# Working the borders between stages in two halves of 128 tokens

## The chip, the cores and the metric

The kernel runs on one core of one Trainium2 chip. The metric is the device time of one execution in microseconds (us); the lower, the better. TensorE multiplies matrices, VectorE (DVE), ScalarE (ACT) and GpSimd (POOL) work elementwise, SyncE (SP) issues the transfers.

## What is computed

The reference is a chain of transformer blocks in float32 on 256 tokens of 1024 channels, with 256 context tokens beside them in the first layer and a half. Cut to what matters here:

```python
def mod_norm(x, m, i, g):
    return rms_norm(x, g) * (1 + m[:, 3 * i + 1, None]) + m[:, 3 * i, None]
def swiglu(h, w1, w2):
    a, b = jnp.split(h @ w1, 2, axis=-1)
    return (jax.nn.silu(a) * b) @ w2
def ffn_sublayer(x, m, i, g, w1, w2):
    return x + HALF_STEP * m[:, 3 * i + 2, None] * swiglu(mod_norm(x, m, i, g), w1, w2)
...
        x = x + m[:, 5, None] * y
        x = ffn_sublayer(x, m, 2, norm_g[l, 2], ffn_w_in[l, 1], ffn_w_out[l, 1])
    return rms_norm(x, final_g)
```

So every stage ends with an output map that adds to the residual x, and the next one begins with a norm of x over its channels and a map of the normed values. After the second layer's last feed-forward part x is normed by `final_g` and normed again by the second block, whose residual is the normed x: this is the doubled norm below. A second block (retention and sparse attention) and a product-key expert layer follow.

## The kernel before

Tokens are the columns of a tile and channels its partitions: x is `X`, eight tiles of 128 channels by T tokens, where T is 512 (256 tokens and 256 of the context) up to the second layer's mixer, and 256 from there on. A linear map goes by output tiles of 128 channels. For each, the 128x1024 weights (a unit) come through the class `Stream`: `load` (L234) issues the transfer on SP, `split` (L240) makes two float32r parts of it, a copy on ScalarE (L252) and a subtraction on VectorE or POOL (L256, L254), and `take` and `next` hand it out. `take` also sets the mark (`busy`) behind which split buffers are free again. `mm3` (L296) issues three matmuls for each 128x128 block of weights: high part by high part of the input (L298), high by low (L299), low by high (L300). So an output tile is 24 matmuls with 8 blocks of weights, and each matmul loads its 128x128 weights anew. Engines work off their instructions in the order in which the program issues them; no scheduler reorders them.

Between two stages stands what is called a border here. `tail` (L716) works the eight output tiles of a stage and evacuates each into x (`evac`, L727: x plus gate times PSUM). Where the tail is the last of its stage, `sq` (L601) squares each x tile on ScalarE (L613) and POOL adds the squares up (L615), `stats` (L617) sums them over the channels by float32 matmuls with one moving column (L623, L624), `rpow` (L645) takes the power -1/2 on VectorE and POOL, `bcast` (L638) spreads the result over the partitions by a 128x128 matmul (L643), and `chunks` (L668) makes the normed input of the next map for each channel tile: `ht` (L659, VectorE), `Hh` (L661, ScalarE), `Hl` (L664, VectorE). Then `group` (L676) starts the next map's first three or four output tiles together, channel tile by channel tile, so that TensorE can begin as soon as the first chunk is there.

With T = 512, `tail` runs the tiles 5 to 7 in two halves of 256 tokens and puts the first half's statistics, broadcast and chunks beside the matmuls of the second; `group` does the same with the second half's. With T = 256 there are no halves: after the eighth tile the branch at L760 splits the units ahead, squares tile 7, and issues statistics, broadcast and all eight chunks one after another; `group` runs one pass of 256 columns.

Three borders have T = 256. The first goes from the second layer's mixer output map (eight blocks of input) to its feed-forward part (three tiles in the group; two more split buffers, m0 and m1, are there). The second goes from the last output map of that feed-forward part (seven blocks) to the second block's mixer (three tiles), with the doubled norm: `sq` squares each tile twice, `stats` takes two powers one after the other, and each chunk also rescales x (L663). The third goes from the second block's output map (eight blocks) to the expert layer's queries (four tiles). In the second and third there are five split buffers.

The branch for T = 256 at the end of `tail`, and the loop of `group`:

```python
        if T == 256:
            W.busy = W.pos
            W.split(W.pos + 4)
            W.load(W.pos + 6)
            self.sq(7)
            self.stats(0)
            self.bcast(0)
            self.chunks(0, 0, KD)
            return
...
        for half in range(T // S):
            if half == T // S - 1:
                W.split(W.pos + W.split_ahead)
```

Of the kernel before, what the change touches and what calls it, by code (L numbers as in the profile page):

```python
# [16 lines left out]
P = 128  # L17
# [269 lines left out]
class Build:  # L287
# [13 lines left out]

    def x_(self, T, d, half=None):
        return self.X[:, :, d, :] if T == 512 and half is None else self.X[:, half or 0, d, :]

    def h_(self, T, k, half=None):
        return [H[:, :, k, :] if T == 512 and half is None else H[:, half or 0, k, :] for H in (self.Hh, self.Hl)]

    def g_(self, T, k, half=None):
        c = slice(0, T) if half is None else slice(half * S, half * S + S)
        return [G[:, k, c] for G in (self.Gh, self.Gl)]  # L310

    def bank_(self, b, T, half=None):
        if isinstance(b, tuple):
            b, half = b
        return self.bank[b][:, :T] if half is None else self.bank[b][:, half * S:half * S + S]
# [285 lines left out]
    def sq(self, d, half=None):  # L601
        nc, T = self.nc, self.nT
        x = self.x_(T, d, half)
        sl = slice(0, T) if half is None else slice(half * S, half * S + S)
        jobs = [(sl, 1.0)]
        if self.ndouble:
            jobs.append((slice(S, 2 * S), self.gn[:, 48 + d:49 + d]))
# [9 lines left out]
    def stats(self, half):  # L617
        nc = self.nc
        st = self.bank[6][:, half * 8:half * 8 + 4]
        nset = 4 if self.ndouble else 2  # L620
        for j in range(nset):
            c0 = half * S + j * P
            nc.tensor.matmul(st[:, j:j + 1], self.nacc[:, c0:c0 + P], self.C["ones"][:, 0:1], start=True, stop=False)  # L623
            nc.tensor.matmul(st[:, j:j + 1], self.nlast[:, c0:c0 + P], self.C["ones"][:, 0:1], start=False, stop=True)  # L624
        ms = self.sm.tile([P, 8], F32, name="ms", tag="ms")
        r = self.sm.tile([P, 8], F32, name="rstd", tag="rstd")
        self.rpow(r[:, 0:2], ms[:, 0:2], st[:, 0:2], 1.0 / D)
        order = [0, 1]
        if self.ndouble:
            nc.vector.tensor_tensor(ms[:, 2:4], r[:, 0:2], r[:, 0:2], OP.mult)  # L630
            nc.vector.tensor_tensor(ms[:, 4:6], ms[:, 2:4], st[:, 2:4], OP.mult)
            self.rpow(r[:, 2:4], ms[:, 6:8], ms[:, 4:6], 1.0 / D)
            nc.vector.tensor_tensor(r[:, 2:4], r[:, 2:4], r[:, 0:2], OP.mult)
            order = [2, 3, 0, 1]
        R = self.bank[7]
        self.nrow[half] = R[:, half * S:half * S + S], [r[:, o:o + 1] for o in order]

    def bcast(self, half):  # L638

        R, cols = self.nrow[half]  # L640
        rows = [R[:, :P], R[:, P:]] + ([self.bank[7][:, S + j * P:S + (j + 1) * P] for j in range(2)] if self.ndouble else [])
# [9 lines left out]
    def chunk(self, half, k):  # L651
# [5 lines left out]
        t = self.np.tile([P, S], F32, name="ht", tag="ht", bufs=3)  # L657
# [4 lines left out]
        if self.ndouble:  # L662
            nc.vector.scalar_tensor_tensor(x, x, self.gn[:, 48 + k:49 + k], self.bank[7][:, S:], op0=OP.mult, op1=OP.mult)  # L663
# [10 lines left out]


    def group(self, labels, T, early=False):  # L676
# [7 lines left out]
        for half in range(T // S):  # L684
            if half == T // S - 1:
                W.split(W.pos + W.split_ahead)
            for k in range(KD):
# [4 lines left out]
                if T == 512 and half == 0:  # L692
# [3 lines left out]
                    if k == 5:  # L696
                        if not early:
                            self.bcast(1)
                        self.chunks(1, 0, KD)
        return bs  # L700
# [15 lines left out]
    def tail(self, label, nk, T, gate, last=True, order=None, rest=None):  # L716
# [3 lines left out]
        def evac(b, d, half):  # L720
# [5 lines left out]
            g = gate(half or 0)  # L726
# [15 lines left out]
        nfull = 5 if last and T == 512 else 8  # L742
# [1150 lines left out]
```

## Time and profile before

| what | value |
|---|---|
| median of 3 runs | 2723.25 us (2722.06 to 2727.45) |
| the profiled execution: its time | 2724.21 us |
| the profiled execution: span of its instructions | 2722.3 us |
| TensorE busy | 97% of the span |
| weight loads busy | 85% |
| VectorE, ScalarE, POOL busy | 65%, 40%, 19% |
| mean granted TensorE clock | 0.991 |

The span is read in the trace from the first instruction to the last; the 1.9 us between it and the time of the same execution lie around it. Matmuls are pipelined and their ends are modelled, so what a matmul costs is read from the distance between the starts of two of them. In a timeline row the numbers are start and length in us, then engine, line, operation, output and input, weights (rows*columns), moving operand (partitions x columns), and in brackets the idle time of the engine before it and what ended it.

### The profile page before, as it was taken

How to read it: one execution, taken by the hardware profiler on the slowest of the kernel's cores; microseconds unless marked ns; L12 is line 12 of the kernel's file. 1: busy time of each engine (PE TensorE's matmuls, PEld its weight loads, DVE VectorE, ACT ScalarE, POOL GpSimd, SP SyncE). 2: the span in 40 equal slices, each digit the busy share in tenths (PEclk: the TensorE clock that was granted, in tenths of full speed). 3: DMA queues.
4: the chain of work that ended last, by engine and by line, in shares of the span. 5: the costliest groups of instructions: out<-in, count | busy, mean ns of one | idle time of the engine just before them, and what ended most of it. 6: DMA issues, size and time to landing. Idle time of an engine off the chain costs nothing. (4 is left out here: it accounts for less than half of the span.)

```text
span 2722.3 us, 40945 instructions
## 1 busy us (share of the span) xinstructions
PE 2639.4 (97%) x15899; PEld 2312.6 (85%) x15899; DVE 1759.6 (65%) x3389; ACT 1102.2 (40%) x1867; POOL 507.7 (19%) x284
## 2 busy tenths in 40 slices
PE   6999999999999999999998999989999999999998
PEld 4888888688888898888978999778999999988887
DVE  6877865557777565555546656775795566655555
ACT  5322234534222242222354445553444545454554
POOL 1000011120000010000122001332697666300000
PEclk9999999999999999999999999999999999999999
DMA  6655643234566535655344655524555444566664
GB/s 246 200 188 182 205 151 111 67 101 140 193 189 194 182 124 186 203 190 194 108 149 130 191 188 172 174 75 160 171 165 169 151 151 148 157 196 204 193 193 140
DMA packets 129476, 451.40 MB, mean 166 GB/s; under 512 B 16000, under 2 KB 21120, under 8 KB 127744
## 3 DMA queue, kind: packets, MB, share of 16 engines
q1 hardware_dynamic: 129280, 448.77, 51.4%
q8 instruction: 125, 2.05, 0.3%
q14 instruction: 71, 0.58, 0.1%
HBM read 446.35 MB, written 2.10 MB: 165 GB/s over the span
## 5 line engine op out<-in xcount | busy, mean ns | idle before, releaser
L298 PE MATMUL bank<-Hh,hl 128*128 128x256 f32 (+1 forms) x1968 | 661.4, 336 | 9.4 <-ACT Hh L661 5.1
L300 PE MATMUL bank<-Hh,hl 128*128 128x256 f32 (+1 forms) x1968 | 639.9, 325 | 4.1 <-POOL hl L254 4.1
L299 PE MATMUL bank<-Hl,hl 128*128 128x256 f32 (+1 forms) x1968 | 640.4, 325 | 0.8 <-DVE Hl L664 0.7
L252 ACT ACTIVATE hl<-raw 128x1024 fp32r<-128x1024 f32 (+1 forms) x401 | 410.9, 1041 | 276.4 <-DMA raw<-in_w_dram 84.1
L256 DVE TENSOR_TENSOR hl<-raw,hl 128x1024 fp32r<-128x1024 f32 (+1 forms) x316 | 383.1, 1222 | 180.2 <-ACT hl L252 177.2
L298 PEld LDWEIGHTS bank<-Hh,hl 128*128 128x128 f32 x1968 | 375.8, 191 | 48.5 <-issue 7.7
L300 PEld LDWEIGHTS bank<-Hh,hl 128*128 128x128 f32 x1968 | 375.2, 191 | 35.2 <-POOL hl L254 4.9
L299 PEld LDWEIGHTS bank<-Hl,hl 128*128 128x128 f32 x1968 | 375.8, 191 | 30.7 <-DVE Hl L664 1.8
L512 DVE SCALAR_TENSOR_TENSOR junk<-wm,cb 128x1024 bf16<-128x1024 f32 x272 | 332.1, 1221 | 11.0 <-ACT cb L518 7.6
L615 POOL TENSOR_TENSOR nacc<-nlast,nacc 128x256 f32<-128x256 f32 (+1 forms) x56 | 60.7, 1089 | 1320.3 <-issue 834.4
L254 POOL TENSOR_TENSOR hl<-raw,hl 128x1024 fp32r<-128x1024 f32 x85 | 212.8, 2507 | 163.1 <-ACT hl L252 157.7
L298 PE MATMUL bank<-G,hl 128*128 128x512 f32 (+1 forms) x673 | 227.6, 338 | 0.0
L300 PE MATMUL bank<-G,hl 128*128 128x512 f32 (+1 forms) x673 | 226.8, 337 | 0.0
L299 PE MATMUL bank<-G,hl 128*128 128x512 f32 (+1 forms) x673 | 226.8, 337 | 0.0
L324 ACT ACTIVATE G<-silu 128x512 fp32r<-128x512 f32 (+1 forms) x88 | 51.1, 580 | 407.1 <-DVE silu L801 407.1
L1841 PE MATMUL bank<-hl,Hh 128*128 128x512 f32 x768 | 179.5, 390 | 0.0
L801 DVE TENSOR_TENSOR silu<-silu,bank 128x512 f32<-128x512 f32 (+1 forms) x88 | 54.6, 621 | 189.1 <-PE bank L300 184.0
L298 PE MATMUL bank<-Hh,hm 128*128 128x512 f32 (+1 forms) x496 | 175.5, 354 | 0.0
L299 PE MATMUL bank<-Hl,hm 128*128 128x512 f32 (+1 forms) x496 | 175.3, 353 | 0.0
L300 PE MATMUL bank<-Hh,hm 128*128 128x512 f32 (+1 forms) x496 | 175.3, 353 | 0.0
L1841 PEld LDWEIGHTS bank<-hl,Hh 128*128 128x128 f32 x768 | 144.3, 188 | 29.8
L727 DVE SCALAR_TENSOR_TENSOR X<-bank,mall,X 128x256 f32<-128x256 f32 x192 | 84.5, 479 | 125.8 <-PE bank L300 125.7
(370 smaller groups left out, 5061.9 us busy)
## 6 DMA issues: line engine op xcount, KB each, us to landing
raw<-in_w_dram SPq DMA_DIRECT2D x208, 512.0 KB, 4.1
wm<-in_wmod_dram SPq DMA_DIRECT2D x128, 512.0 KB, 4.3
X<-in_wdn_dram SPq DMA_DIRECT2D x64, 512.0 KB, 3.6
raw<-in_wdn_dram SPq DMA_DIRECT2D x64, 512.0 KB, 3.6
X<-in_wup_dram SPq DMA_DIRECT2D x64, 512.0 KB, 3.6
raw<-in_wup_dram SPq DMA_DIRECT2D x64, 512.0 KB, 3.6
raw<-in_w_dram SPq DMA_DIRECT2D x64, 448.0 KB, 3.9
wm<-in_wada_dram SPq DMA_DIRECT2D x48, 512.0 KB, 4.6
```

The costliest lines, as they stand in the source:

```text
L252: nc.scalar.activation(hl[:, 0, :n], raw[:, :n], AF.Copy)
L254: nc.gpsimd.tensor_tensor(hl[:, 1, :n], raw[:, :n], hl[:, 0, :n].bitcast(F32), OP.subtract)
L256: nc.vector.tensor_tensor(hl[:, 1, :n], raw[:, :n], hl[:, 0, :n].bitcast(F32), OP.subtract)
L298: mm(o, wh, xh, start=start, stop=False)
L299: mm(o, wh, xl, start=False, stop=False)
L300: mm(o, wl, xh, start=False, stop=stop)
L324: nc.scalar.activation(dst[0], src, AF.Copy)
L512: nc.vector.scalar_tensor_tensor(junk, w, 1.0, self.cb[c], op0=OP.mult, op1=OP.mult, accum_out=o)
L615: self.nadd.tensor_tensor(acc, last, acc, OP.add)
L727: nc.vector.scalar_tensor_tensor(x, self.bank_(b, T, half), g[:, d:d + 1], x, op0=OP.mult, op1=OP.add)
L801: nc.vector.tensor_tensor(s, s, self.bank_(bb, T), OP.mult)
L1841: nc.tensor.matmul(acc[t][n], c[:, a, ts], u[:, b, n * 512:(n + 1) * 512], start=e == 0 and a + b == 0, stop=e == P - 1 and a == 1)
```

## The change

At the three borders with T = 256 the work goes in two halves of 128 tokens, as it does with two halves of 256 tokens where T = 512. `part` cuts x, `Hh` and `Hl` into halves; `tail` runs only the tiles 0 to 4 whole and the tiles 5 to 7 in halves, and the branch for T = 256 is gone; `stats` and `bcast` take one column of 128 tokens each time (two with the doubled norm); `group` always runs two halves, with the second half's statistics, chunks and broadcast between the matmuls of the first. `rescale` takes the rescaling of x out of the chunks and issues it, eight instructions of 256 columns, after the group. The units ahead are no longer split before the chunks with `W.busy = W.pos`, but as many as find a buffer at the three tiles' `take`, and the rest in `group`'s `take`.

```diff
+    def part(self, A, T, k, half):
+
+        if T == 512:
+            return A[:, :, k, :] if half is None else A[:, half, k, :]
+        return A[:, 0, k, :] if half is None else A[:, 0, k, half * P:(half + 1) * P]
...
     def stats(self, half):
...
-        nset = 4 if self.ndouble else 2
-        for j in range(nset):
-            c0 = half * S + j * P
+        hs = self.nT // 2
+        n = hs // P
+        cols = [half * hs + j * P for j in range(n)]
+        if self.ndouble:
+            cols += [S + c for c in cols]
+        for j, c0 in enumerate(cols):
...
     def chunk(self, half, k):
...
-        if self.ndouble:
-            nc.vector.scalar_tensor_tensor(x, x, self.gn[:, 48 + k:49 + k], self.bank[7][:, S:], op0=OP.mult, op1=OP.mult)
...
+    def rescale(self):
+
+        for k in range(KD):
+            x = self.x_(self.nT, k)
+            self.nc.vector.scalar_tensor_tensor(x, x, self.gn[:, 48 + k:49 + k], self.bank[7][:, S:], op0=OP.mult, op1=OP.mult)
...
     def group(self, labels, T, early=False):
...
-        for half in range(T // S):
-            if half == T // S - 1:
+        for half in range(2):
+            if half == 1:
                 W.split(W.pos + W.split_ahead)
...
-                if T == 512 and half == 0:
+                if half == 0:
...
+        if self.ndouble:
+            self.rescale()
...
     def tail(self, label, nk, T, gate, last=True, order=None, rest=None):
...
-        nfull = 5 if last and T == 512 else 8
+        nfull = 5 if last else 8
...
-        if T == 256:
-            W.busy = W.pos
-            W.split(W.pos + 4)
-            W.load(W.pos + 6)
-            self.sq(7)
-            self.stats(0)
-            self.bcast(0)
-            self.chunks(0, 0, KD)
-            return
         us = W.take([(*label, d) for d in range(5, 8)])
         W.split(W.pos + 3)
         W.load(W.pos + 6)
```

How the instructions stand is shown at three places. The first is TensorE at the third border, from the last output tile (`bank_66<-G`) to the next map's first tile (`bank_63<-Hh`); `bank_69` holds the statistics and `bank_70` the broadcast. Before:

```order
L300 MATMUL bank_66<-G,hl_93 128x256
L623 MATMUL bank_69<-con_79,nacc 128x1
L624 MATMUL bank_69<-con_79,nlast 128x1
L623 MATMUL bank_69<-con_79,nacc 128x1
L624 MATMUL bank_69<-con_79,nlast 128x1
L643 MATMUL bank_70<-con_79,rstd 128x128 x2
L298 MATMUL bank_63<-Hh,hl_77 128x256
L299 MATMUL bank_63<-Hl,hl_77 128x256
```

Now, where the first half's broadcast stands, between the second halves of tile 6 (`bank_68`) and tile 7 (`bank_66`):

```order
L299 MATMUL bank_68<-G,hl_92 128x128
L300 MATMUL bank_68<-G,hl_92 128x128
L654 MATMUL bank_70<-con_79,rstd 128x128
L298 MATMUL bank_66<-G,hx 128x128
L299 MATMUL bank_66<-G,hx 128x128
```

Statistics and broadcast, which stood alone between the two maps, have moved among the matmuls of the tail (and, for the second half, of the group); each matmul of tiles 5 to 7 and of the group stands twice with 128 columns where it stood once with 256.

The second place is ScalarE at the third border, from the last squares of the tail (`nlast<-X`) to the chunks (`Hh<-ht`). `L252 ... hl_78<-raw_90` and `hl_92<-raw_74` are the copies of the group's third and fourth unit. Before:

```order
L613 ACTIVATE nlast<-X 128x256
L252 ACTIVATE hl_78<-raw_90 128x1024
L613 ACTIVATE nlast<-X 128x256
L252 ACTIVATE hl_92<-raw_74 128x1024
L613 ACTIVATE nlast<-X 128x256
L661 ACTIVATE Hh<-ht,mad_80 128x256 x8
L252 ACTIVATE Hh<-X 128x1024
```

Now:

```order
L619 ACTIVATE nlast<-X 128x128 x4
L672 ACTIVATE Hh<-ht,mad_80 128x128 x4
L619 ACTIVATE nlast<-X 128x128 x2
L672 ACTIVATE Hh<-ht,mad_80 128x128 x2
L252 ACTIVATE hl_78<-raw_90 128x1024
L252 ACTIVATE hl_92<-raw_74 128x1024
L672 ACTIVATE Hh<-ht,mad_80 128x128 x10
```

The copies of the third and fourth unit have moved from ahead of all chunks to behind six chunks of the first half.

The third place is VectorE at the same border: the evacuations of tile 6 and 7 (L727, now L744), the subtractions of the same two units (L256), the step to the power (`ms`) and the chunks. Before:

```order
L727 SCALAR_TENSOR_TENSOR X<-bank_68,mad_80,X 128x256
L256 TENSOR_TENSOR hl_78<-raw_90,hl_78 128x1024
L727 SCALAR_TENSOR_TENSOR X<-bank_66,mad_80,X 128x256
L256 TENSOR_TENSOR hl_92<-raw_74,hl_92 128x1024
L647 TENSOR_SCALAR ms<-bank_69 128x2
L659 SCALAR_TENSOR_TENSOR ht<-X,mad_80,bank_70 128x256 x2
L664 SCALAR_TENSOR_TENSOR Hl<-ht,mad_80,Hh 128x256
```

Now:

```order
L744 SCALAR_TENSOR_TENSOR X<-bank_68,mad_80,X 128x128
L744 SCALAR_TENSOR_TENSOR X<-bank_66,mad_80,X 128x128
L670 SCALAR_TENSOR_TENSOR ht<-X,mad_80,bank_70 128x128 x2
L673 SCALAR_TENSOR_TENSOR Hl<-ht,mad_80,Hh 128x128 x2
L256 TENSOR_TENSOR hl_78<-raw_90,hl_78 128x1024
L256 TENSOR_TENSOR hl_92<-raw_74,hl_92 128x1024
L658 TENSOR_SCALAR ms<-bank_69 128x1
```

The two subtractions stand behind the last evacuation and six chunks of the first half now, and ahead of the second half's power. At the second border the group's third unit (`hx<-raw_74`) has moved in the same way; at the first border all three units are split ahead of the chunks as before.

## Rows read from the trace of the kernel before

**Rows 1.** The page: busy time of the engines, their share of the span, instructions.

```profile
PE 2639.4 (97%) x15899; PEld 2312.6 (85%) x15899; DVE 1759.6 (65%) x3389; ACT 1102.2 (40%) x1867; POOL 507.7 (19%) x284
```

**Rows 2.** Timeline, TensorE, 256 columns: two matmuls 24 apart.

```profile
1483.89 0.28 PE L298 MATMUL bank<-G,hl 128*128 128x256 f32 x1
...
1486.71 0.28 PE L298 MATMUL bank<-G,hl 128*128 128x256 f32 x1
```

**Rows 3.** Timeline (start, length, idle before), TensorE, first border.

```profile
1486.95 0.28 PE L300 MATMUL bank<-G,hl 128*128 128x256 f32 x1
...
1492.00 0.38 PE L298 MATMUL bank<-Hh,hl 128*128 128x256 f32 x1 [1.12 <-ACT Hh L661]
...
1495.85 0.28 PE L299 MATMUL bank<-Hl,hm 128*128 128x256 f32 x1
```

**Rows 4.** Timeline, TensorE, second border.

```profile
1678.67 0.28 PE L300 MATMUL bank<-G,hm 128*128 128x256 f32 x1
...
1687.53 0.58 PE L298 MATMUL bank<-Hh,hl 128*128 128x256 f32 x1 [1.11 <-ACT Hh L661]
...
1693.83 0.28 PE L298 MATMUL bank<-Hh,hl 128*128 128x256 f32 x1
```

**Rows 5.** Timeline, TensorE, third border.

```profile
1864.19 0.28 PE L300 MATMUL bank<-G,hl 128*128 128x256 f32 x1
...
1869.39 0.58 PE L298 MATMUL bank<-Hh,hl 128*128 128x256 f32 x1 [1.11 <-ACT Hh L661]
...
1874.85 0.28 PE L298 MATMUL bank<-Hh,hl 128*128 128x256 f32 x1
```

**Rows 6.** Windows: us, busy us (x count) of PE, PEld, DVE, ACT, POOL, TensorE clock, DMA.

```profile
1687.50:1693.00 5.50, 4.77 (x20) 4.48 (x21) 5.36 (x13) 2.03 (x4) 0.00 (x0) 0.50 0.07 23
...
1869.40:1874.60 5.20, 5.20 (x23) 4.97 (x24) 5.18 (x13) 3.26 (x7) 0.00 (x0) 0.50 0.00 0
```

**Rows 7.** Timeline, TensorE: 64 weight columns, 128 moving columns, and the next row.

```profile
1795.45 1.04 PE L1470 MATMUL bank<-X,VT 128*64 128x128 f32 x16
1796.43 0.39 PE L298 MATMUL bank<-Hh,hl 128*128 128x256 f32 x1
```

**Rows 8.** Timeline, TensorE: float32 in two passes, 128 weight columns, 128 moving columns.

```profile
1800.50 0.38 PE L1518 MATMUL bank<-RV,rs 128*128 128x128 f32 x2
...
1800.94 0.39 PE L1520 MATMUL bank<-RV,rs 128*128 128x128 f32 x2
```

**Rows 9.** Timeline, TensorE: the same with one moving column, five apart.

```profile
1680.28 0.36 PE L623 MATMUL bank<-con,nacc 128*128 128x1 f32 x2
...
1681.39 0.36 PE L624 MATMUL bank<-con,nlast 128*128 128x1 f32 x2
```

**Rows 10.** Groups by form, weight loads: count, busy us, mean ns, idle before.

```profile
L298 PEld LDWEIGHTS bank<-Hh,hl 128*128 128x128 f32 x1968 | 375.8, 191 | 48.5 <-issue 7.7 <-ACT Hh L661 6.0 <-ACT Q L890 2.3
...
L1307 PEld LDWEIGHTS bank<-hl,G 128*60 128x60 f32 x56 | 6.6, 132 | 0.5
```

**Rows 11.** Timeline, second border: from the statistics to the broadcasts.

```profile
1681.80 0.16 DVE L647 TENSOR_SCALAR ms<-bank 128x2 f32<-128x2 f32 x1 [1.19 <-PE bank L624]
...
1684.34 0.58 PE L643 MATMUL bank<-con,rstd 128*128 128x128 f32 x1 [2.59 <-DVE rstd L633]
```

**Rows 12.** Groups by form, ScalarE: copy of a split, Hh of a chunk, square.

```profile
L252 ACT ACTIVATE hl<-raw 128x1024 fp32r<-128x1024 f32 x357 | 371.3, 1053 | 253.4 <-PE bank L1841 83.8 <-DMA raw<-in_w_dram 83.2 <-PE bank L299 32.4
...
L661 ACT ACTIVATE Hh<-ht,mall 128x256 fp32r<-128x256 f32 x88 | 42.7, 506 | 50.0 <-DVE ht L659 50.0
...
L613 ACT ACTIVATE nlast<-X 128x256 f32<-128x256 f32 x45 | 18.7, 416 | 51.3 <-DVE X L727 37.5 <-POOL nacc L615 13.8
```

**Rows 13.** Groups by form, VectorE: subtraction of a split, evacuation.

```profile
L256 DVE TENSOR_TENSOR hl<-raw,hl 128x1024 fp32r<-128x1024 f32 x272 | 336.0, 1244 | 174.8 <-ACT hl L252 172.9 <-PE bank L1095 1.7
...
L727 DVE SCALAR_TENSOR_TENSOR X<-bank,mall,X 128x256 f32<-128x256 f32 x192 | 84.5, 479 | 125.8 <-PE bank L300 125.7
```

**Rows 14.** Timeline, weight loads of twelve float32 matmuls with four rows.

```profile
44.10 0.92 PEld L494 LDWEIGHTS bank<-con,row 4*128 4x128 f32 x12 [2.38 <-DVE row L489]
```

More of the change, by code (lines that the diff above doesn't have):

```diff
@@ L300, in mm3 @@
         mm(o, wl, xh, start=False, stop=stop)
+    def part(self, A, T, k, half):
+        if T == 512:
+            return A[:, :, k, :] if half is None else A[:, half, k, :]
+        return A[:, 0, k, :] if half is None else A[:, 0, k, half * P:(half + 1) * P]
     def x_(self, T, d, half=None):
-        return self.X[:, :, d, :] if T == 512 and half is None else self.X[:, half or 0, d, :]
+        return self.part(self.X, T, d, half)
     def h_(self, T, k, half=None):
-        return [H[:, :, k, :] if T == 512 and half is None else H[:, half or 0, k, :] for H in (self.Hh, self.Hl)]
+        return [self.part(H, T, k, half) for H in (self.Hh, self.Hl)]
     def g_(self, T, k, half=None):
-        c = slice(0, T) if half is None else slice(half * S, half * S + S)
+        c = slice(0, T) if half is None else slice(half * T // 2, (half + 1) * T // 2)
         return [G[:, k, c] for G in (self.Gh, self.Gl)]
@@ L313, in bank_ @@
         if isinstance(b, tuple):
-            b, half = b
-        return self.bank[b][:, :T] if half is None else self.bank[b][:, half * S:half * S + S]
+            return self.bank[b[0]][:, b[1] * S:b[1] * S + S]
+        return self.bank[b][:, :T] if half is None else self.bank[b][:, half * T // 2:(half + 1) * T // 2]
     def next_bank(self):
@@ L603, in sq @@
         x = self.x_(T, d, half)
-        sl = slice(0, T) if half is None else slice(half * S, half * S + S)
+        sl = slice(0, T) if half is None else slice(half * T // 2, (half + 1) * T // 2)
         jobs = [(sl, 1.0)]
         if self.ndouble:
-            jobs.append((slice(S, 2 * S), self.gn[:, 48 + d:49 + d]))
+            jobs.append((slice(S + sl.start, S + sl.stop), self.gn[:, 48 + d:49 + d]))
         for sl, sc in jobs:
@@ L626, in stats @@
         r = self.sm.tile([P, 8], F32, name="rstd", tag="rstd")
-        self.rpow(r[:, 0:2], ms[:, 0:2], st[:, 0:2], 1.0 / D)
-        order = [0, 1]
+        self.rpow(r[:, 0:n], ms[:, 0:n], st[:, 0:n], 1.0 / D)
+        order = list(range(n))
         if self.ndouble:
[L630 to L634, printed above, removed]
+            nc.vector.tensor_tensor(ms[:, 2:3], r[:, 0:1], r[:, 0:1], OP.mult)
+            nc.vector.tensor_tensor(ms[:, 4:5], ms[:, 2:3], st[:, 1:2], OP.mult)
+            self.rpow(r[:, 2:3], ms[:, 6:7], ms[:, 4:5], 1.0 / D)
+            nc.vector.tensor_tensor(r[:, 2:3], r[:, 2:3], r[:, 0:1], OP.mult)
+            order = [2, 0]
         R = self.bank[7]
-        self.nrow[half] = R[:, half * S:half * S + S], [r[:, o:o + 1] for o in order]
+        self.nrow[half] = R[:, half * hs:(half + 1) * hs], [r[:, o:o + 1] for o in order]
     def bcast(self, half):
         R, cols = self.nrow[half]
-        rows = [R[:, :P], R[:, P:]] + ([self.bank[7][:, S + j * P:S + (j + 1) * P] for j in range(2)] if self.ndouble else [])
+        rows = [R[:, j * P:(j + 1) * P] for j in range(self.nT // S)]
+        if self.ndouble:
+            rows.append(self.bank[7][:, S + half * P:S + (half + 1) * P])
         for o, c in zip(rows, cols):
@@ L656, in chunk @@
         R = self.nrow[half][0]
-        t = self.np.tile([P, S], F32, name="ht", tag="ht", bufs=3)
+        t = self.np.tile([P, S], F32, name="ht", tag="ht", bufs=3)[:, :T // 2]
         x = self.x_(T, k, half)
@@ L725, in evac @@
             x = self.x_(T, d, half)
-            g = gate(half or 0)
+            g = gate(half or 0 if T == 512 else 0)
             nc.vector.scalar_tensor_tensor(x, self.bank_(b, T, half), g[:, d:d + 1], x, op0=OP.mult, op1=OP.add)
```

1 line of the change is left out of this document (added).

## The prediction

> **What bounds the kernel now.** I began with the page's busy times: TensorE is busy for 97% of the span and no other engine is near [rows 1]. So the question at a border is only how long TensorE needs from the tail's last tiles to the end of the group, idle time included. I read that next, from the timeline of TensorE at each border. A matmul of 256 columns at full pace takes (1486.71 - 1483.89) / 24 = 0.1175 us [rows 2].
>
> What a border loses is the time from its last tail matmul to a matmul of the group that runs at full pace again, less the matmuls between at 0.1175 us. At the first border the 17th matmul after the last of the tail starts 8.90 us later, and 17 x 0.1175 = 2.0: 6.9 us lost [rows 3]. At the second the 25th starts 15.16 us later, less 2.94: 12.2 us [rows 4]. At the third the 25th starts 10.66 us later: 7.7 us [rows 5]. In all 26.8 us. One part of it is the gap in which TensorE waits for squares, statistics, power, broadcast and the first chunk; what ends it is the first chunk's `Hh` (the releaser in the brackets [rows 3, 4, 5]). The other part follows: after the gaps at the second and third border the granted clock is 0.50, that is 1.2 GHz, for the next 5.5 and 5.2 us; in the second of these windows 23 matmuls took 5.20 us, 0.226 each [rows 6].
>
> So 26.8 us (1% of the span) is the most that the change can win. What it pays with is matmuls of half the size. An output tile is 24 matmuls (21 in the second border's tail, with seven blocks), so tiles 5 to 7 have 72, 63 and 72 at the three borders, and the groups of 3, 3 and 4 tiles 72, 72 and 96. These 447 matmuls of 256 columns become 894 of 128.
>
> **What a half costs.** No row before has a float32r matmul of 128 moving columns with 128 weight columns, so I bound it. From below: float32 passes of 128 moving columns over only 64 weight columns take 0.98 / 16 = 0.061 us each [rows 7]. There the moving columns set the pace. From above: the same with 128 weight columns takes 0.44 / 2 = 0.22 us for two passes, 0.111 a pass [rows 8], and with a single moving column it is again (1681.39 - 1680.28) / 5 / 2 = 0.111 [rows 9]. A price that does not change between 1 and 128 moving columns is not that of the columns; it doubles with the weight columns, so it is the weight load's. A float32r load has the same nature in the trace: 191 ns with 128 columns and 132 with 60 [rows 10], 59 ns for 68 columns, or 0.87 ns a column and 111 ns for 128. Halves load the same weights as wholes did. **I take 0.111 us for a half, almost as much as the whole of 0.1175**: it is the row nearest in form, and the load's own slope gives the same. The ends for the range are 0.061 and 0.1175.
>
> The Trainium skill, TensorE: Matmul & The Clock Gate, section Back-to-back issue gap, would have it otherwise: about 81 ns for each pair of load and matmul with 128 columns, and N / 2.4 + 2.5 ns, 56 ns, for a matmul that stands alone. No run here shows either; 0.111 with one moving column [rows 9] speaks against both for float32 weights. By 81 ns the 894 halves would cost 72 us and not 99, by 56 ns 50 us.
>
> **The sum, border by border.** A pass of statistics or broadcast is 0.111 us too. Such passes stood in the lost time before, and now stand in TensorE's stream.
> - First border. 288 halves x 0.111 = 32.0, and 12 passes 1.3: 33.3 us. Before, 144 x 0.1175 + 6.9 = 23.8. **+9.5 us.** All three units are split ahead, so I charge no wait: between the last evacuation and the need for the second half's chunks lie 72 halves of the group's first half, 8 us.
> - Second border. 270 halves = 30.0, 24 passes 2.7. The chain with two powers took 2.54 us from the statistics to the broadcast [rows 11]; beside it run 21 halves of tile 6, 2.3 us, so with handovers 0.5 is left over. Then a new stall. The group's third unit is split only behind the last squares and six chunks, on both engines. After the tail's last matmul come the evacuation, two squares, two `Hh`, the copy (1.05) [rows 12] and the subtraction (1.24) [rows 13]. With 256 columns an evacuation takes 0.48 [rows 13], a square 0.42 and an `Hh` 0.51 [rows 12]; for 128, which no row shows, I take 0.35, 0.35 and 0.40, between half and whole. That is 0.35 + 0.70 + 0.80 + 1.05 + 1.24 = 4.1, against 8 halves (0.9) that TensorE can do before it needs the low part: 3.25, with handovers 3.5 us. Between ends of 0 (if a buffer comes free sooner) and 7. For the clock after it I charge 1.0, between 0 (TensorE stays busier than in rows 3) and 2.6 (half of the 5.2 us of rows 5). Sum 37.7, before 135 x 0.1175 + 12.2 = 28.1. **+9.6 us.**
> - Third border. 336 halves = 37.3, 12 passes 1.3. Here the third and the fourth unit are late: 0.35 + 0.35 + 0.80 + 1.05 + 2 x 1.24 = 5.0 less 11 halves (1.2), with handovers 4.1; clock 1.0. Sum 43.7, before 168 x 0.1175 + 7.7 = 27.4. **+16.3 us.**
>
> All other edits together I cost at nothing. The eight rescalings of 256 columns (no longer than an evacuation, 0.48 [rows 13], so under 4 us of VectorE) follow the group's chunks and lie beside its second half, 72 halves or 8 us, and the next single tile; without that cover they would delay the first evacuations of the new stage by up to 4 us. The shorter statistics and chunk instructions double in number, beside TensorE's stream. On SP one load of a unit at the second border moves behind two loads of constants; the unit is used after the group only, over 8 us later. POOL's nine more additions lie beside the tail.
>
> Sum: +9.5 + 9.6 + 16.3 = +35.4 us, or as one line: 894 x 0.111 = 99.2, and 15.4 for the rest (passes 5.3, chain 0.5, late splits 7.6, clock 2.0), against 79.3 now. Against the profiled execution of 2724.21 us (1.9 us of it outside its span) that is 2759.6. The median is 0.96 us lower: 2758.7. **I forecast 2759 us**: what the halves hide (26.8) is less than what they add (894 x 0.111 - 447 x 0.1175 = 46.7).
>
> **Rivals.** The price of a half decides, at 63.9 / 894 = 0.0715 us: below it the change wins.
> - *The columns set the price* (the faster side). If float32r weights go in beside the running matmul, a half costs 0.061: 54.5 + 15.4 - 79.3 = -9.4. The cover shrinks with it: 21 halves are 1.3 us against a chain of 2.54, so 0.8 more at the second border, and about 0.9 more for the second half's power. -7.7, about 2716. For it: whole matmuls do hide loads of 191 ns behind 117 ns [rows 2, 10]. Against it: the one-column rows [rows 9], and loads of 0.87 ns a column. Chance 0.08. By the Trainium skill's lone gap of 56 ns (same section) it would be 2711 or so.
> - *Loads as fast as the fastest seen.* Twelve loads of 128 columns with four rows took 0.92 us, 0.077 each [rows 14]. Then 68.8 + 15.4 - 79.3 = +4.9: 2728, within what can be told. Against it: four rows are not 128. Chance 0.06.
> - *A load half hidden*, midway between 0.061 and 0.111 at 0.086: +13.0, 2736. Chance 0.06. The Trainium skill's 81 ns (same page and section) would give +8.5, 2732, by the same mechanism.
> - *A half pays two loads*, as a two-pass float32 matmul of 128 columns does, 0.22 us [rows 8]: 198.5 + 15.4 - 79.3 = +135, 2858. For it is only that the type is kin; the wholes at 0.1175 show one pass. Chance 0.03.
>
> **How the numbers follow.** Forecast 0.77, the rivals 0.08, 0.06, 0.06 and 0.03. A measurement of this kernel can tell about 0.2%, 5.4 us, from no change. Faster holds the first rival, 0.08; the second is within, 0.06; forecast, third and fourth are slower, 0.86. The forecast's own ends: without late splits, clock and chain 99.2 + 5.3 - 79.3 = +25, 2748; at 0.1175 a half with the clock at its upper end (5.2) 105.0 + 5.3 + 0.5 + 7.6 + 5.2 - 79.3 = +44, and a late split a third longer +47, 2771. The range takes in the half-hidden load with some play, and reaches from 2732 to 2771; this leaves out the first two rivals, the last and little of the forecast's own.
>
> **What would show it.** In the profile of the changed kernel: starts of the 128-column rows of the three `mm3` lines 0.111 us apart in the tails' last tiles and in the groups; no gap of 5 us at any border, but waits of 3 to 4 us before the third unit at the second and third, none at the first; a border-to-border time of 33, 38 and 44 us; the rescaling's rows beside busy TensorE. The forecast is wrong if those starts stand 0.06 to 0.09 apart, or if TensorE's idle time at the borders is more than some 10 us in sum.

## The result, and the profile after

The changed kernel takes 2797.78 us (median of 4 runs, 2795.55 to 2801.21) against 2724.35 of the kernel before on the same chips: ratio 1.0273, 95% interval 1.0261 to 1.0286. (Ratios here and below are to the kernel before.) It is slower, as forecast, but by 73 us and not by 35; 2797.78 lies outside the range of 2732 to 2771. The profiled execution's span grew from 2722.3 to 2793.7 us, 71.4.

The page and the cores' view of the changed kernel answer to [rows 1]:

```profile
span 2793.7 us, 41961 instructions
PE 2719.8 (97%) x16346; PEld 2393.5 (86%) x16346; DVE 1769.5 (63%) x3453; ACT 1109.5 (40%) x1903; POOL 510.5 (18%) x296
core 0: 2793.7 us, clock 0.978
```

TensorE is as busy as before, 97% of a longer span, and its mean granted clock went from 0.991 to 0.978. The windows of the three borders tell where (us, busy us of PE, PEld, DVE, ACT, POOL, then the TensorE clock and the DMA share); they answer to [rows 6]:

```profile
1475.92:1509.37 33.45, 33.45 (x302) 33.45 (x301) 19.44 (x49) 15.73 (x31) 5.58 (x8) 1.00 0.29 95
1678.47:1691.00 12.53, 12.53 (x115) 12.53 (x113) 4.50 (x11) 3.90 (x10) 5.52 (x9) 1.00 0.43 127
1692.00:1732.30 40.30, 38.34 (x179) 37.96 (x179) 17.18 (x50) 10.54 (x25) 2.60 (x6) 0.50 0.23 81
1890.76:1908.00 17.24, 17.24 (x157) 17.24 (x156) 7.52 (x19) 5.16 (x11) 4.68 (x6) 1.00 0.48 175
1911.00:1953.20 42.20, 41.40 (x192) 41.02 (x192) 10.48 (x25) 7.69 (x15) 0.56 (x1) 0.50 0.18 63
```

The first border (1475.92, the first half of tile 5, to 1509.37, the first single tile behind the group) never leaves the full clock. The second (1678.47 to 1732.30) and the third (1890.76 to 1953.26) lose it midway and then run 40 and 42 us at 0.50, 1.2 GHz, with TensorE busy nearly all of that time. Two pairs of rows of TensorE's timeline show the price of a half at either clock, 19 matmuls apart in the first border, and 89 apart in the second:

```profile
1476.88 0.28 PE L298 MATMUL bank<-G,hl 128*128 128x128 f32 x1
...
1479.00 0.27 PE L299 MATMUL bank<-G,hl 128*128 128x128 f32 x1
...
1713.06 0.45 PE L298 MATMUL bank<-Hh,hl 128*128 128x128 f32 x1
...
1732.09 0.41 PE L300 MATMUL bank<-Hh,hx 128*128 128x128 f32 x1
```

(1479.00 - 1476.88) / 19 = 0.112 us at full clock, as taken in the prediction, and (1732.09 - 1713.06) / 89 = 0.214 at the lower one.

| border | before | forecast | measured |
|---|---|---|---|
| first | 23.8 | 33.3 | 33.45 |
| second | 28.1 | 37.7 | 53.8 |
| third | 27.4 | 43.7 | 62.5 |
| sum | 79.3 | 114.7 | 149.8 |

The borders give 70.5 us of the span's 71.4. At 0.50 stood 165 halves of the second border and 186 of the third: 351 x (0.214 - 0.111) = 36 us, about the whole of what the forecast missed.

Where the clock fell at the second border the rows are the statistics of the first half (four matmuls of two passes, one moving column), 21 halves, and the broadcast, behind which the spacing is 0.21:

```profile
1687.80 0.33 PE L632 MATMUL bank<-con,nacc 128*128 128x1 f32 x2
1687.99 0.36 PE L633 MATMUL bank<-con,nlast 128*128 128x1 f32 x2
1688.22 0.36 PE L632 MATMUL bank<-con,nacc 128*128 128x1 f32 x2
1688.44 0.36 PE L633 MATMUL bank<-con,nlast 128*128 128x1 f32 x2
...
1691.14 1.22 PE L654 MATMUL bank<-con,rstd 128*128 128x128 f32 x4
1692.02 0.45 PE L298 MATMUL bank<-G,hm 128*128 128x128 f32 x1
1692.27 0.41 PE L299 MATMUL bank<-G,hm 128*128 128x128 f32 x1
```

No row there shows TensorE idle. The waits for the late units come after that at the second border, and at the third they stand at the fall:

```profile
1699.41 0.47 PE L298 MATMUL bank<-Hh,hx 128*128 128x128 f32 x1 [1.39 <-ACT hx L252]
...
1700.67 0.47 PE L300 MATMUL bank<-Hh,hx 128*128 128x128 f32 x1 [0.57 <-DVE hx L256]
...
1910.91 0.48 PE L298 MATMUL bank<-Hh,hl 128*128 128x128 f32 x1 [2.63 <-ACT hl L252]
...
1912.17 0.48 PE L300 MATMUL bank<-Hh,hl 128*128 128x128 f32 x1 [0.57 <-DVE hl L256]
...
1913.31 0.47 PE L300 MATMUL bank<-Hh,hl 128*128 128x128 f32 x1 [0.23 <-DVE hl L256]
```

### The profile page after: what moved, and what is told of

The parts are those of the page before. It is cut to its first block, busy times and chain, and to the rows that moved or that the text cites. A ratio compares the mean times of both kernels' runs of the same rounds, so it can differ in the third digit from the quotient of the medians.

```text
span 2793.7 us, 41961 instructions
## 1 busy us (share of the span) xinstructions
PE 2719.8 (97%) x16346; PEld 2393.5 (86%) x16346; DVE 1769.5 (63%) x3453; ACT 1109.5 (40%) x1903; POOL 510.5 (18%) x296
## 4 chain that ended last, share of the span: by engine, by line
PE 90%; DVE 4%; ACT 2%; issue 2%; DMA 1%; POOL 1%; SPq 0%; POOLq 0%; DVEq 0%; ACTq 0%
PE bank L298 23%; PE bank L300 23%; PE bank L299 23%; PE bank L1849 12%; PE bank L1690 2%; PE bank L1072 1%; PE bank L1118 1%; PE bank L1103 1%; PE bank L893 1%; PE bank L892 1%; PE bank L894 1%; DVE G L331 0%; ACT hl L252 0%; DVE hl L256 0%; POOL hl L254 0%
## 5 line engine op out<-in xcount | busy, mean ns | idle before, releaser
L298 PE MATMUL bank<-Hh,hl 128*128 128x256 f32 (+2 forms) x2040 | 692.2, 339 | 7.5 <-ACT hl L252 2.6
L300 PE MATMUL bank<-Hh,hl 128*128 128x256 f32 (+2 forms) x2040 | 670.4, 329 | 4.9 <-POOL hl L254 4.1
L299 PE MATMUL bank<-Hl,hl 128*128 128x256 f32 (+2 forms) x2040 | 670.3, 329 | 0.9 <-DVE Hl L673 0.9
L252 ACT ACTIVATE hl<-raw 128x1024 fp32r<-128x1024 f32 (+1 forms) x401 | 409.9, 1039 | 286.5 <-PE bank L1849 83.9
L256 DVE TENSOR_TENSOR hl<-raw,hl 128x1024 fp32r<-128x1024 f32 (+1 forms) x318 | 383.5, 1217 | 179.5 <-ACT hl L252 177.0
L298 PEld LDWEIGHTS bank<-Hh,hl 128*128 128x128 f32 x2040 | 401.1, 197 | 46.1 <-issue 8.1
L300 PEld LDWEIGHTS bank<-Hh,hl 128*128 128x128 f32 x2040 | 400.4, 196 | 36.4 <-POOL hl L254 4.9
L299 PEld LDWEIGHTS bank<-Hl,hl 128*128 128x128 f32 x2040 | 401.2, 197 | 30.4 <-DVE Hl L673 1.2
L621 POOL TENSOR_TENSOR nacc<-nlast,nacc 128x256 f32<-128x256 f32 (+2 forms) x64 | 61.2, 961 | 1335.7 <-ACT nlast L619 676.0
L298 PE MATMUL bank<-G,hl 128*128 128x512 f32 (+2 forms) x719 | 239.7, 333 | 0.0
L300 PE MATMUL bank<-G,hl 128*128 128x512 f32 (+2 forms) x719 | 238.7, 332 | 0.0
L299 PE MATMUL bank<-G,hl 128*128 128x512 f32 (+2 forms) x719 | 238.7, 332 | 0.0
L298 PE MATMUL bank<-Hh,hm 128*128 128x512 f32 (+2 forms) x512 | 179.2, 350 | 0.0
L299 PE MATMUL bank<-Hl,hm 128*128 128x512 f32 (+2 forms) x512 | 179.0, 350 | 0.0
L300 PE MATMUL bank<-Hh,hm 128*128 128x512 f32 (+2 forms) x512 | 179.0, 350 | 0.0
L744 DVE SCALAR_TENSOR_TENSOR X<-bank,mall,X 128x256 f32<-128x256 f32 (+1 forms) x198 | 85.6, 471 | 124.5 <-PE bank L300 124.4
```

Of the source, the lines that this page charges most:

```text
L252: nc.scalar.activation(hl[:, 0, :n], raw[:, :n], AF.Copy)
L256: nc.vector.tensor_tensor(hl[:, 1, :n], raw[:, :n], hl[:, 0, :n].bitcast(F32), OP.subtract)
L298: mm(o, wh, xh, start=start, stop=False)
L299: mm(o, wh, xl, start=False, stop=False)
L300: mm(o, wl, xh, start=False, stop=stop)
L621: self.nadd.tensor_tensor(acc, last, acc, OP.add)
```

## The experiments

A half is a matmul of 128 moving columns here, a whole one of 256. The theory after the result (W): a wait amid halves brings the clock down, and halves do not bring it back, though wholes did so within 6.3 us of their first in the kernel before [rows 3, 4, 5]. Its rivals: halves by themselves pull the clock down (H), or a late unit costs its wait alone. For the second border's fall without a wait a separate theory (S): the one-column passes do it.

### No late unit

```diff
-            b4, b5, b6 = self.group([("win2f", f) for f in (4, 5, 6)], T)
+            b4, b5 = self.group([("win2f", f) for f in (4, 5)], T)
+            b6 = self.lin(("win2f", 6), T)
...
-            self.pq = self.group([("wpq", f) for f in range(4)], T)
+            self.pq = self.group([("wpq", f) for f in range(2)], T) + [self.lin(("wpq", f), T) for f in (2, 3)]
```

> The changed kernel, but the groups at the second and third border take only two units; the third (and fourth) output tile follows alone, in wholes of 256 columns. So no unit is split late. Theory W (the clock fell at the third border because TensorE waited 2.6 us for the late third unit, and once at 1.2 GHz the halves keep it there): the third border runs at a granted clock of 1.00 throughout and takes 240 halves x 0.111 + 12 passes + 48 wholes x 0.1175 = 33.6 us, not 62.5; the second border still falls where it fell (at its statistics, before any late unit), so the total is about 2797.8 - 29 - 8 = 2761. Theory H (halves by themselves pull the clock down after some time, with or without a wait): the third border falls as well, about 50 us, total 2775 to 2790.

Measured: 2760.61 us, ratio 1.0132 (1.0113 to 1.0150). The windows of the third border's halves, and of the second's behind its broadcast:

```profile
1886.11:1914.27 28.16, 28.16 (x254) 28.16 (x253) 15.81 (x45) 12.12 (x28) 5.69 (x8) 1.00 0.30 106
...
1696.00:1723.80 27.80, 27.80 (x132) 27.80 (x132) 17.57 (x51) 11.06 (x25) 2.18 (x5) 0.50 0.35 115
```

Without the wait the third border keeps the full clock through all 240 halves, 28.16 us, and with 48 wholes (5.6) it takes 33.8: H falls, W's number stands. The second still falls right behind its statistics, without a wait in it.

### Statistics with 128 moving columns

```diff
+        w = P if self.nT == 256 else 1
...
+            o, one = (st[:, j * w:j * w + w], self.C["ones"][:, :w])
-            nc.tensor.matmul(st[:, j:j + 1], self.nacc[:, c0:c0 + P], self.C["ones"][:, 0:1], start=True, stop=False)
+            nc.tensor.matmul(o, self.nacc[:, c0:c0 + P], one, start=True, stop=False)
```

(and the same for `nlast`, with `st` as wide as is needed).

> The changed kernel, but the statistics' matmuls of the three borders with 256 tokens have 128 moving columns of ones in place of one; by the rows of the kernel before, both take 0.222 us, so only the columns that TensorE multiplies differ. Theory S (at the second border the clock falls at 1691 us because of the four one-column matmuls of the doubled norm, 0.9 us with hardly a column): the clock stays at 1.00 past the second border's broadcast, and falls there, if at all, at the wait for the late third unit; that border is 5 to 16 us shorter than 53.8. The third border as in the changed kernel, 62.5 us. Total 2782 to 2793. Rival (the broadcast's wait or the halves alone do it): the clock falls at the same place, second border 53.8 us, total 2798.

Measured: 2796.91, ratio 1.0265 (1.0246 to 1.0284). The windows of the second border's tail and of its group, and between them the wait for the late unit:

```profile
1679.68:1695.30 15.62, 15.57 (x141) 15.43 (x139) 6.74 (x19) 5.70 (x16) 6.43 (x11) 1.00 0.32 98
1700.00:1732.50 32.50, 31.93 (x151) 31.74 (x150) 12.60 (x36) 6.31 (x14) 1.09 (x2) 0.50 0.21 76
```

```profile
1699.60 0.48 PE L298 MATMUL bank<-Hh,hx 128*128 128x128 f32 x1 [3.48 <-ACT hx L252]
```

The clock no longer falls at the broadcast, as S has it for this pair of runs; a run below shows that S is not the whole of it. But TensorE, now ahead of ScalarE, waits 3.48 us for the late unit in place of 1.39 and falls there. So the border is only 1 us shorter (1679.68 to 1732.50), below the 5 us that I had as the least: what was won at the statistics went into a longer wait.

### Both together, and the wait that was left

The edits of the two runs above in one kernel.

> The two edits together: no late unit, and statistics of 128 columns. Theory W with S: the granted clock is 1.00 at all three borders, 33.4 us at the first, about 30.6 at the second (222 halves, 24 passes, 24 wholes, 0.5 of chain), 33.6 at the third, against 23.8, 28.1 and 27.4 in the kernel before: +18.3, total 2742.5. Theory H: at least one border still falls to 1.2 GHz; total above 2760.

Measured: 2752.00, ratio 1.0099 (1.0083 to 1.0114), 9.5 us above the number. Windows of the second border ahead of the second half's broadcast and behind it, and the broadcast's row:

```profile
1679.22:1700.00 20.78, 20.74 (x184) 20.50 (x182) 9.46 (x30) 7.90 (x22) 7.97 (x15) 1.00 0.38 121
1702.00:1714.00 12.00, 12.00 (x59) 12.00 (x59) 11.03 (x28) 7.06 (x13) 0.00 (x0) 0.51 0.37 113
```

```profile
1701.19 0.71 PE L656 MATMUL bank<-con,rstd 128*128 128x128 f32 x4 [1.12 <-DVE ht L672]
```

With two units in the group, 18 halves (2.0 us) stand between the second half's statistics and its broadcast, too few for the chain of two powers. A wait of 1.12 us amid halves was followed by the fall. I tried twice to take it away by order: first with the broadcast one channel tile later.

```diff
-                    if k == 5:
+                    if k == (6 if self.ndouble and len(us) == 2 else 5):
```

> As the run with two units and wide statistics together, but at the second border the second half's broadcast stands behind the group's seventh channel tile in place of the sixth, so that 24 halves and not 18 lie beside the chain of two powers. In that run TensorE waited 1.2 us there and fell to 1.2 GHz. Theory W (a wait amid halves brings the fall, and halves then keep the clock down): no wait, granted clock 1.00 at all three borders, second border 9 us shorter; total 2743, which is the price of the halves alone. Rival: the clock falls at the second border nevertheless; total 2750 or more.

Measured: 2753.24, ratio 1.0107. A miss: the wait moved to the group's seventh channel tile, ended by that chunk's `Hh`, which stands behind the chain of powers on VectorE:

```profile
1702.25 0.33 PE L298 MATMUL bank<-Hh,hl 128*128 128x128 f32 x1 [1.30 <-ACT Hh L674]
```

Then with those chunks ahead of the statistics:

```diff
+                    short = self.ndouble and len(us) == 2
+                    if k == 1 and short:
+                        self.chunks(0, 6, KD)
+                        self.stats(1)
-                    if k == 2 and not early:
+                    if k == 2 and not early and not short:
```

> As the run with two units and wide statistics together, with the group at the second border in another order: the chunks 6 and 7 of the first half stand ahead of the second half's statistics on VectorE (behind them they waited for the two powers), and the statistics behind the group's second channel tile in place of the third. Theory W: no wait of 1 us at the second border, granted clock 1.00 at all three borders, second border about 31 us; total 2743, the price of halves, passes and wholes alone. Rival: the clock falls there once more, total 2750 or above.

Measured: 2752.43, ratio 1.0101, another miss. The statistics now came too early (0.42 us of waiting for POOL's sum of squares), and the broadcast waited 1.31 for the second power:

```profile
1701.55 1.13 PE L656 MATMUL bank<-con,rstd 128*128 128x128 f32 x4 [1.31 <-DVE rstd L644]
```

The chain is longer than the cover that either order gave it. So I left the wait as it was in the run "both", and filled it:

```diff
+                        if self.ndouble:
+                            self.fill(14)
...
+    def fill(self, n):
+        for _ in range(n):
+            self.nc.tensor.matmul(self.bank[self.ring[0]][:, :S], self.Gh[:, 0, :P], self.Gh[:, 1, :S], start=True, stop=True)
```

> As the run with two units and wide statistics together, with 14 matmuls of 256 columns whose result nobody reads (1.6 us) ahead of the second half's broadcast at the second border, where that run waited 1.2 us and fell to 1.2 GHz; nothing else. Theory W: granted clock 1.00 at all three borders. The 60 halves behind the broadcast take 6.7 us and not 12.4, and the wholes behind them 2.8 us less: 2744, though TensorE does 14 matmuls more. That is the price of the halves without any fallen clock, +20 against the kernel before. Rival (a wait costs its own length only): 2752 or a little more, as in that run.

Measured: 2745.32, ratio 1.0087 (1.0069 to 1.0105). The windows of the three borders' halves:

```profile
1478.16:1511.61 33.45, 33.45 (x303) 33.45 (x301) 19.48 (x49) 15.75 (x31) 5.65 (x8) 1.00 0.31 95
1680.71:1710.29 29.58, 29.53 (x263) 29.37 (x261) 16.33 (x52) 13.68 (x35) 8.37 (x15) 1.00 0.36 117
1869.83:1897.99 28.16, 28.16 (x254) 28.16 (x253) 15.81 (x45) 12.09 (x28) 5.71 (x8) 1.00 0.30 105
```

Full clock at all three borders. TensorE does 14 matmuls more than in the run "both" and the kernel is 6.7 us faster (the kernel before took 2723.63 beside the one and 2722.17 beside the other); the second border's halves take 29.58 us in place of 34.82. By the span it stands 2743.5 - 2722.3 = 21.2 us above the kernel before (by the medians 23.2): that is what this kernel's 750 halves, its wider statistics and the 14 matmuls cost where the clock does not fall. The change itself has 894 halves; its price at full clock and without waits was not measured.

### The other way round: a late unit at the first border

```diff
+        if label[0] == "wout" and T == 256:
+            W.cap = W.pos + 5
         us = W.take([(*label, d) for d in range(5, 8)])
...
         self.chunks(0, 4, 6)
+        W.cap = 10 ** 6
```

(`split` stops at `cap`.)

> The changed kernel with one unit split late at the first border too: the split of the group's third unit is held back until behind six chunks, as the change has it at the second border. Nothing else. Theory W: TensorE waits 1.5 to 3 us for it, the clock falls to 0.50 there and stays until the group's last half; about 130 halves at 0.2135 in place of 0.111 and the wait: +15 to +17 us, total 2813. Rival (the late unit costs its wait only): +2 to +3 us, total 2800.

Measured: 2815.51 (ratio 1.0338, 1.0319 to 1.0357), 17.7 above the changed kernel. The late unit's row and the windows ahead of it and behind it:

```profile
1497.32 0.33 PE L299 MATMUL bank<-Hh,hm 128*128 128x128 f32 x1 [2.63 <-ACT hm L253]
```

```profile
1474.00:1495.00 21.00, 20.69 (x185) 20.55 (x183) 9.61 (x23) 7.18 (x15) 6.73 (x9) 1.00 0.43 142
1499.00:1528.70 29.70, 29.70 (x141) 29.70 (x141) 9.46 (x25) 8.30 (x15) 0.56 (x1) 0.50 0.26 90
```

A wait of 2.6 us (and one of 0.8 behind it) turned the border that kept the clock into one like the other two: it took 51.77 us (1477.16 to 1528.93) in place of 33.45.

In the traces of the kernels with halves stand ten waits of 1.1 to 3.5 us amid halves at full clock, and at each the clock fell, during the wait or about 1 us behind it at the latest. This run also limits theory S. Its second border has the statistics of one column, as the changed kernel has, at 1708.72 to 1709.72, and yet keeps the full clock as far as the wait for the late unit:

```profile
1708.70:1715.70 7.00, 7.00 (x62) 6.81 (x61) 3.56 (x15) 2.10 (x6) 1.98 (x4) 1.00 0.00 0
...
1712.06 0.71 PE L655 MATMUL bank<-con,rstd 128*128 128x128 f32 x4
...
1719.21 0.33 PE L299 MATMUL bank<-Hh,hx 128*128 128x128 f32 x1 [3.47 <-ACT hx L253]
```

So with one column the clock fell behind the first half's statistics in three kernels (the changed one, the one without a late unit, and the one with the rescaling back), and not in this one; with 128 columns it fell there in none of five. The narrow passes bear on the fall, but they do not always bring it, and what decides is open.

### Halves behind a fall, without the rest of the change

```diff
+        cut = labels[0][:2] == ("w1", 3)
-        for half in range(T // S):
+        for half in range(2 if cut else T // S):
...
+                c = slice(half * P, half * P + P)
+                xh, xl = [H[:, 0, k, c] for H in (self.Hh, self.Hl)] if cut else self.h_(T, k, half)
```

> The kernel before, with nothing but this: the group at the first border works its 72 matmuls of 256 columns as 144 of 128, first all of the first 128 tokens, then the others. The border's gap and the clock's fall behind it stay. Theory W (halves keep a fallen clock down): granted clock 0.50 for all of the 144 halves, 30.7 us, in place of the 10.3 us of the wholes: +20 us, total 2744. Rival (the clock comes back after 3.7 us, as behind the wholes): 17 halves at 0.2135 and 127 at 0.111, 17.8 us: +7.5, total 2731.

Measured: 2747.53 (ratio 1.0089, 1.0070 to 1.0107), +24 against the 20 expected. First and last half of the group, and the windows of the group and of the wholes behind it:

```profile
1493.21 0.47 PE L298 MATMUL bank<-Hh,hl 128*128 128x128 f32 x1 [1.11 <-ACT Hh L661]
...
1524.08 0.41 PE L300 MATMUL bank<-Hh,hm 128*128 128x128 f32 x1
```

```profile
1493.20:1524.30 31.10, 31.04 (x145) 30.86 (x145) 8.38 (x17) 6.97 (x11) 0.00 (x0) 0.50 0.16 51
1524.30:1534.00 9.70, 9.70 (x66) 9.70 (x67) 6.31 (x12) 4.34 (x7) 0.00 (x0) 0.76 0.21 63
```

144 halves in 30.9 us, all at 0.50; where wholes follow, the clock rises (at 1528.9, 4.6 us after the first of them). In the kernel before, the wholes of the same group brought it back 3.85 us after their first [rows 3]. That is W's second part by itself. What the 24 us have beyond the expected 20 stands at the group's two ends: the gap ahead of it was 7.5 us and not 5.05, as ScalarE's copy of a unit waited 2.77 us for its transfer, and the wholes behind it began at the lower clock.

### The rescaling back in the chunks

```diff
+        if self.ndouble:
+            nc.vector.scalar_tensor_tensor(x, x, self.gn[:, 48 + k:49 + k], self.bank[7][:, S + half * P:S + half * P + P], op0=OP.mult, op1=OP.mult)
...
-        if self.ndouble:
-            self.rescale()
```

> The changed kernel with the rescaling back in the chunks, half by half (sixteen instructions of 128 columns in place of eight of 256 behind the group). Both theories: within 1 us of the changed kernel at the second border (53.8 us), since VectorE has idle time there: the rescaling's new place is worth nothing. If it had been the rescaling that delays the new stage, the time would fall by 1 to 4 us.

Measured: 2799.36 against 2797.78, and the second border takes 54.2 us against 53.8. The rescaling's new place is worth nothing here, as costed. Both kernels run this border at 0.50; at full clock it was not tried.

### A version that beats both: the kernel before, with its gaps filled

Three runs put matmuls into the gaps of the kernel before, the first two with one-column statistics.

```diff
+            n = (7, 20, 8) if self.ndouble else (8, 8, 8)
             self.sq(7)
+            self.fill(n[0])
             self.stats(0)
+            self.fill(n[1])
             self.bcast(0)
+            self.fill(n[2])
             self.chunks(0, 0, KD)
```

In the first, `fill` writes `self.bank[6][:, S:]`, beside the statistics.

> The kernel before with matmuls of 256 columns whose result nobody reads in the three gaps of each border: 8 ahead of the statistics, 8 (second border 20) ahead of the broadcast, 8 ahead of the group. Nothing else is moved. If the clock's fall after a gap is what the second part of a border's loss was, the clock stays at 1.00 after the gaps and each border is shorter by half of the 3.7, 5.5 and 5.2 us that ran at 1.2 GHz: -7 us, ratio 0.997. Rival: the fill delays the statistics and the broadcast behind it as much as it saves: same time or +1 to +3 us.

Measured: 2723.53 against 2723.63, ratio 1.0000 (0.9991 to 1.0009). No gain in spite of 7 us expected. The clock stayed at the first and the third border, but the second lost what they won. There the clock is 1.00 from 1674.00 to 1677.50, as long as the sixteen one-column passes run, and 0.50 from 1677.60 to 1684.30; and the fill ahead of the broadcast stood behind VectorE's reading of the statistics in the same bank:

```profile
1678.98 4.64 PE L647 MATMUL bank<-G 128*128 128x256 f32 x20 [1.42 <-DVE ms L631]
```

The second run writes the bank that the group takes next, as `fill` above does.

> The kernel before with the matmuls that fill the gaps, as in the run before, but into the bank that the group writes next anyway, not into the half of the statistics' bank: there the fill waited for VectorE's reading of the statistics (1.42 us at the second border). Theory: granted clock 1.00 behind all three gaps, no wait of the fill for VectorE; -1.5, -3 and -2 us at the borders, total 2717, ratio 0.998. Rival: equal to the kernel before within 1 us, because the fill delays what stands behind it.

Measured: 2720.05 against 2723.40, ratio 0.9988 (0.9979 to 0.9997). There is no such wait any more. The clock still fell behind the second border's sixteen one-column passes, though for half as long. Windows of these passes and of the fill behind them:

```profile
1675.20:1677.40 2.20, 2.07 (x20) 1.98 (x18) 1.13 (x1) 0.82 (x2) 0.00 (x0) 1.00 0.74 222
1677.50:1680.80 3.30, 3.30 (x16) 3.30 (x17) 0.81 (x5) 0.00 (x0) 1.40 (x2) 0.50 0.93 364
```

The third adds the statistics of 128 columns.

(In the third run the statistics' columns stand in a whole bank, 128 for each.)

> As the second run with filled gaps, with 128 moving columns of ones in the statistics: in that run the clock fell at the second border during its 16 one-column passes. Theory S: granted clock 1.00 at all three borders; 2 us less than that run (2720.1), 2718, ratio to the kernel before 0.998. Rival: the clock falls there with 128 columns too: 2720.

Measured: 2719.34 against 2724.84, ratio 0.9981 (0.9972 to 0.9990): the fastest kernel of this study. Windows of the same length behind the last tail matmul, first the kernel before, then this one:

```profile
1486.95:1498.95 12.00, 8.75 (x58) 8.19 (x57) 8.97 (x20) 6.42 (x12) 0.70 (x1) 0.86 0.29 92
1678.70:1692.70 14.00, 8.82 (x46) 7.94 (x45) 8.48 (x22) 3.54 (x8) 2.19 (x4) 0.67 0.56 199
1864.20:1876.00 11.80, 8.69 (x49) 8.00 (x48) 8.63 (x20) 5.65 (x11) 0.70 (x1) 0.71 0.30 103
```

```profile
1485.00:1497.00 12.00, 11.62 (x93) 10.89 (x92) 8.94 (x20) 5.97 (x11) 0.70 (x1) 1.00 0.28 88
1677.00:1691.00 14.00, 12.70 (x96) 11.35 (x95) 9.19 (x23) 3.94 (x9) 2.18 (x4) 1.00 0.58 199
1861.20:1873.00 11.80, 11.42 (x92) 10.71 (x91) 8.74 (x20) 6.12 (x12) 0.70 (x1) 1.00 0.28 100
```

The gap from the last tail matmul to the group's first is about as long as before at the first and third border (5.2 us each against 5.05 and 5.2) and 0.8 us shorter at the second; what changed is the clock, 1.00 in place of 0.86, 0.67 and 0.71. The second and the third filled kernel differ little in time (2720.05 and 2719.34, intervals that overlap), so what the wider statistics add by themselves is told by the clock, not by the times.

## Why the prediction was wrong

**What held.** The price of a half was the step that I rested the most on, and it was right: 0.112 us against 0.111. The one-column rows [rows 9] and the slope of the weight loads [rows 10] had told it. So were the counts: the first border came out at 33.45 where 33.3 was forecast. The forecast's direction and its reason (halves pay the full weight load, and what they add is more than the gaps lose) are borne out by the run that keeps the full clock at its borders: with 750 halves in place of 375 wholes and 14 matmuls of filling it is still +21.2 us by the span. The Trainium skill, TensorE: Matmul & The Clock Gate, section LDWEIGHTS (loading the stationary operand), puts a load at columns / 1.2 ns, 107 ns for 128; at full clock the trace agrees within 5 ns, at 0.50 a half takes twice that. Its section Back-to-back issue gap, with 81 or 56 ns, does not agree with any stretch of halves here.

**What failed.** The term of the clock: "For the clock after it I charge 1.0, between 0 ... and 2.6" at the second border, and 1.0 again at the third. The upper end is half of the 5.2 us of the third border [rows 5, 6], where wholes follow the gap and bring the clock back. (At the second border they need 6.3 us by [rows 4]; the window of 5.5 us in [rows 6] stops before the rise.) I took over such a length for a stretch of halves. The runs show another mechanism in its place: halves hold a full clock (33 us at the first border) but do not win back a fallen one, so the loss is not a fixed few us but every half that is left, 165 and 186 of them, 36 us in all. The run with halves only in the group shows the second part alone, the one with a late unit at the first border the whole chain. Why halves hold a clock that they do not win back, no run here tells.

**The late units** were foreseen in kind and mis-sized as a cost. As waits they were shorter than charged (2.0 and 3.4 us against 3.5 and 4.1). At the second border that is because TensorE came late, at the lower clock: in the kernel with wide statistics, which reaches the late unit at full clock, it waited 3.48 and 0.57, some 4.1 us. As the trigger at the third border they cost far more: without them it took 33.8 us in place of 62.5, and of these 28.7 only 5.0 come from 48 wholes in place of 96 halves (96 x 0.111 - 48 x 0.1175).

**The second border** fell ahead of any wait, which the prediction did not have at all. Its doubled norm's one-column passes, which I had costed as 0.111 each and nothing else, bear on it: two pairs of kernels that differ in those columns differ in the clock (the changed kernel and the one with wide statistics; the second and the third filled kernel). They are not the whole cause, since the run with a late unit at the first border kept the clock behind the same passes. Nor did they decide this border's time: with the fall there gone it was 1 us shorter, as the late unit brought the fall instead.

**What would have shown it wrong** was named as starts 0.06 to 0.09 apart or idle time above 10 us in sum. Neither came: the starts stand 0.112 and 0.214 apart, and TensorE's idle time at the three borders is 5.4 us. Only the border-to-border times, of the signs named for the forecast, told the miss; the loss stands in busy time, at a clock that the window view has in its own column.

**Costed at nothing** and so found: the rescaling. That the moved transfer on SP and POOL's additions cost nothing was not tried by themselves; the first border's agreement within 0.2 us speaks for the additions.

## What to carry to other kernels

Before cutting a matmul's moving columns, look for rows with still fewer columns over the same weights: where they cost the same, as here, expect the weight load to set the price and a half to cost nearly a whole. Where a stretch is paced by weight loads, take care that nothing waits in it: waits of 1 to 3.4 us cost 7 to 24 us here, because the clock came back only with the next wide matmuls. And where a gap can't be closed, a few matmuls for nothing in it can be worth more than hiding it: 5 us here, a fifth of what the gaps seemed to lose.

## What had not been expected of the hardware

- TensorE was busy for over 38 of 40 us at the second border and for 41 of 42 at the third, and the granted clock stayed at 0.50 throughout. The Trainium skill, same page, section HAM oscillation — how this bites in real kernels, ties the lower clock to idle gaps; here it also fell without one (second border, at the broadcast at 1691.14) and stayed low without one.
- Two-pass matmuls with one moving column and with 128 take the same 0.22 us, but eight such passes of one column amid halves were followed by a fall of the clock in three kernels of four, and the same number with 128 columns in none of five.
